# Batch norm with ReLU on one core: storing the second half of x by one DMA of 8 MB instead of two of 4 MB

## Chip, cores and metric

One core of a Trainium2 chip. The metric is device time in microseconds (us), median of several executions.

## The reference

```python
def reference(x, gamma, beta, running_mean, running_var, eps):
    normalized = (x - running_mean[None, :, None, None]) / np.sqrt(running_var[None, :, None, None] + eps)
    scaled = normalized * gamma[None, :, None, None] + beta[None, :, None, None]
    return np.maximum(scaled, 0).astype(np.float32)
```

x is 32 x 128 x 32 x 32 float32, 16.78 MB; the output is as large. Everything else is tiny.

## The kernel before

The 4096 rows (batch times channel) of 1024 numbers are cut into two halves `t`; in a half each of 128 partitions holds 16 consecutive rows `j`, 64 KB, contiguous in HBM. The sync queue loads pieces of a half; ScalarE applies scale, bias and ReLU in place, one row `j` (128 x 1024) an instruction; the scalar queue stores a piece when its rows are done. The scales and biases come from a short chain at the start, cut here.

```python
J = 16
PIECES = (((0, 2), (2, 4), (4, 8), (8, 16)), ((0, 8), (8, 16)))
STORE_CUTS = {(0, 1)}
# ...
    tiles = []
    for t in range(T):
        for a, b in PIECES[t]:
            xt = data.tile([P, b - a, HW], F32, name=f"x{t}_{a}")
            nc.sync.dma_start(out=xt, in_=xr[t, :, a:b, :])
            tiles.append((t, a, b, xt))
# ... scales and biases ...
    with tc.manual_schedule(engines={mybir.EngineType.Activation}):
        for t, a, b, xt in tiles:
            first = a
            for j in range(a, b):
                nc.scalar.activation(out=xt[:, j - a, :], in_=xt[:, j - a, :], func=ACTF.Relu,
                                     bias=bias_t[:, j : j + 1], scale=scale_t[:, j : j + 1])
                if j + 1 == b or (t, j + 1) in STORE_CUTS:
                    nc.scalar.dma_start(
                        out=outr[t, :, first : j + 1, :], in_=xt[:, first - a : j + 1 - a, :])
                    first = j + 1
```

A piece is called by its tile: x0_8 is rows 8 to 15 of the first half, x1_0 and x1_8 are the two pieces of the second. A DMA of n rows moves, on each partition, one run of n x 4 KB.

## Time and profile before

| | before |
|---|---|
| time, median of 3 | 83.86 us (83.7 to 83.93) |
| span of the profiled execution | 81.9 us |
| busy: ScalarE; every other engine | 47%; 1% or less |
| loads, stores | 16.78 MB each |
| share of 16 DMA engines: loads, stores | 48.4%, 47.8% |

The profile's lines are in the prediction, where they are read. Besides its views I use the records of single DMA packets: start, length, size and queue. In this kernel one packet of data is one run on one partition. A record does not name its engine: "on one engine" means packets that follow one another without a pause.

### The profile page before, as it was taken

The numbers are of one execution on the slowest core, as the hardware profiler recorded it, in microseconds if no ns is written. First come the engines' busy times: TensorE is split into PE (matmuls) and PEld (weight loads), VectorE is DVE, ScalarE is ACT, GpSimd is POOL, SyncE is SP. The second block draws the span as 40 slices with busy tenths as digits, with TensorE's granted clock in tenths as the row PEclk, the third lists the DMA queues.
The fourth block names the chain that finished last, engine by engine and source line by source line (L and its number), as shares of the span: only waits on it lengthen the run. The fifth ranks groups of instructions, "written<-read, shape, count | busy, mean of one in ns | idle before, by whom it ended". The sixth has DMA issues, their size and how long they took to land.

```text
span 81.9 us, 119 instructions
## 1 busy us (share of the span) xinstructions
PE 0.7 (1%) x2; PEld 0.5 (1%) x2; DVE 0.8 (1%) x5; ACT 38.5 (47%) x34; POOL 0.8 (1%) x6
## 2 busy tenths in 40 slices
PE   0002000000000000000000000000000000000000
PEld 0002000000000000000000000000000000000000
DVE  0000300000000000000000000000000000000000
ACT  0600377799039999199994199993000000000000
POOL 3000000000000000000000000000000000000000
DMA  2899999989899999979789798996999899799690
GB/s 32 328 425 472 408 448 448 512 352 494 370 448 416 446 418 396 500 296 600 320 380 580 304 464 384 512 512 288 480 512 400 368 512 448 320 512 496 272 512 0
DMA packets 1936, 33.56 MB, mean 410 GB/s; under 512 B 272, under 2 KB 272, under 8 KB 528
## 3 DMA queue, kind: packets, MB, share of 16 engines
q1 hardware_dynamic: 864, 16.78, 48.4%
q10 hardware_dynamic: 1072, 16.78, 47.8%
HBM read 16.78 MB, written 16.78 MB: 410 GB/s over the span
## 4 chain that ended last, share of the span: by engine, by line
DMA 56%; ACT 11%; SPq 0%; issue 0%
DMA x<-in_x_dram 56%; ACT x L96 11%; SPq L52 0%
## 5 line engine op out<-in xcount | busy, mean ns | idle before, releaser
L96 ACT ACTIVATE x<-x,bias_t,scale_t 128x1024 f32<-128x1024 f32 x32 | 37.0, 1228 | 10.3 <-DMA x<-in_x_dram 7.9
L82 ACT ACT_TABLE_LOAD x1 | 1.3, 1283 | 2.6 <-issue 2.6
L82 ACT ACTIVATE std_t<-cols,eps_t 128x16 f32<-128x16 f32 x1 | 0.3, 273 | 4.5 <-PE cols L74 4.5
L74 PE MATMUL cols<-raw,rep 8*128 8x64 f32 x2 | 0.7, 428 | 7.7 <-DMA raw<-in_beta_dram 7.7
L74 PEld LDWEIGHTS cols<-raw,rep 8*128 8x128 f32 x2 | 0.5, 304 | 7.7 <-issue 7.7
L64 POOL TENSOR_SCALAR_AFFINE_SELECT rep<-rep 8x128 f32<-8x128 f32 x1 | 0.4, 392 | 0.1
L84 DVE RECIPROCAL rstd_t<-std_t 128x16 f32<-128x16 f32 x1 | 0.3, 254 | 7.8 <-ACT std_t L82 7.8
L63 POOL MEMSET rep<- 8x128 f32 x1 | 0.2, 195 | 0.3 <-POOLq L124 0.3
L86 DVE TENSOR_TENSOR scale_t<-cols,rstd_t 128x16 f32<-128x16 f32 x1 | 0.2, 175 | 0.1
L90 DVE TENSOR_TENSOR bias_t<-cols,ms_t 128x16 f32<-128x16 f32 x1 | 0.2, 175 | 0.0
L88 DVE TENSOR_TENSOR ms_t<-cols,scale_t 128x16 f32<-128x16 f32 x1 | 0.2, 175 | 0.0
L124 POOL MEMSET const-bfloat16-1.0<- 128x1 bf16 x1 | 0.1, 106 | 0.0
L124 POOL MEMSET const-uint8-127<- 128x1 uint8 x1 | 0.1, 106 | 0.0
L124 POOL MEMSET const-float32-0.0<- 128x1 f32 x1 | 0.1, 103 | 0.3 <-issue 0.3
L124 POOL MEMSET const-float32-1.0<- 128x1 f32 x1 | 0.1, 103 | 0.0
L61 DVE MEMSET eps_t<- 128x1 f32 x1 | 0.1, 59 | 0.9 <-PEq L124 0.9
## 6 DMA issues: line engine op xcount, KB each, us to landing
x<-in_x_dram SPq DMA_DIRECT2D x3, 4096.0 KB, 38.8
out_dram<-x ACTq DMA_DIRECT2D x3, 4096.0 KB, 27.9
x<-in_x_dram SPq DMA_DIRECT2D x2, 1024.0 KB, 5.7
x<-in_x_dram SPq DMA_DIRECT2D x1, 2048.0 KB, 11.2
out_dram<-x ACTq DMA_DIRECT2D x1, 2048.0 KB
out_dram<-x ACTq DMA_DIRECT2D x2, 512.0 KB, 18.8
out_dram<-x ACTq DMA_DIRECT2D x1, 1024.0 KB
raw<-in_running_var_dram ACTq DMA_DIRECT2D x1, 0.5 KB
```

The lines of the kernel that those rows point to most:

```text
L61: nc.vector.memset(eps_t, float(eps))
L63: nc.gpsimd.memset(rep, 1.0)
L64: nc.gpsimd.affine_select(out=rep, in_=rep, compare_op=mybir.AluOpType.is_equal, fill=0.0, base=0, pattern=[[0, P // Q], [-1, Q]], channel ...
L74: nc.tensor.matmul(cols.rearrange("p k j -> p (k j)"), rep.rearrange("q r s -> q (r s)"), raw.rearrange("q k j -> q (k j)"), start=True, s ...
L82: nc.scalar.activation(out=std_t, in_=cols[:, 0, :], func=ACTF.Sqrt, bias=eps_t[:, 0:1], scale=1.0)
L84: nc.vector.reciprocal(out=rstd_t, in_=std_t)
L86: nc.vector.tensor_mul(out=scale_t, in0=cols[:, 1, :], in1=rstd_t)
L88: nc.vector.tensor_mul(out=ms_t, in0=cols[:, 2, :], in1=scale_t)
L90: nc.vector.tensor_sub(out=bias_t, in0=cols[:, 3, :], in1=ms_t)
L96: nc.scalar.activation(out=xt[:, j - a, :], in_=xt[:, j - a, :], func=ACTF.Relu, bias=bias_t[:, j : j + 1], scale=scale_t[:, j : j + 1],)
L124: nc = _bacc.Bacc("TRN2", target_bir_lowering=False, num_devices=1)
```

## The change

Its intent: store the second half with one DMA and longer runs (64 KB in place of 32), so fewer packets and one DMA fewer. The half becomes one tile; its two loads stay, each into a part of it. The store must now wait for all sixteen rows.

```diff
-PIECES = (((0, 2), (2, 4), (4, 8), (8, 16)), ((0, 8), (8, 16)))
+TILES = ((0, 0, 2), (0, 2, 4), (0, 4, 8), (0, 8, 16), (1, 0, 16))
 
+LOAD_CUTS = {(1, 8)}
 STORE_CUTS = {(0, 1)}
@@
-    for t in range(T):
-        for a, b in PIECES[t]:
-            xt = data.tile([P, b - a, HW], F32, name=f"x{t}_{a}")
-            nc.sync.dma_start(out=xt, in_=xr[t, :, a:b, :])
-            tiles.append((t, a, b, xt))
+    for t, a, b in TILES:
+        xt = data.tile([P, b - a, HW], F32, name=f"x{t}_{a}")
+        cuts = [a] + [j for j in range(a + 1, b) if (t, j) in LOAD_CUTS] + [b]
+        for c, d in zip(cuts, cuts[1:]):
+            nc.sync.dma_start(out=xt[:, c - a : d - a, :], in_=xr[t, :, c:d, :])
+        tiles.append((t, a, b, xt))
```

## The prediction

> **What bounds the kernel now.** I began with the page's busy shares, which rule the compute engines out: ScalarE (ACT) is busy 47% of an 81.9 us span, nothing else over 1%. The row of DMA slices and the two queue lines say what is full.
>
> ```profile
> DMA  2899999989899999979789798996999899799690
> DMA packets 1936, 33.56 MB, mean 410 GB/s; under 512 B 272, under 2 KB 272, under 8 KB 528
> q1 hardware_dynamic: 864, 16.78, 48.4%
> q10 hardware_dynamic: 1072, 16.78, 47.8%
> L96 ACT ACTIVATE x<-x,bias_t,scale_t 128x1024 f32<-128x1024 f32 x32 | 37.0, 1228 | 10.3 <-DMA x<-in_x_dram 7.9
> ```
>
> The two queues (q1 loads, q10 stores) fill 48.4 + 47.8 = 96.2% of 16 engines' time; only the first slice and the last one or two are empty. So bytes over rate set the time: 33.56 MB, which the change leaves alone. The question left is whether the changed stores let the engines run dry, make packets slower, or add a tail. The chain of waits names only the loads and the last eight activations, and shows when the second half is ready:
>
> ```profile
> 7.99 38.77 DMA x<-in_x_dram
> 46.76 0.03 issue
> 46.79 9.16 ACT x L96 x8
> ```
>
> Read it with care: it stops at 55.95 us although the span ends at 81.9, since nothing follows the last activation but transfer. The last 26 us are stores. For those I read the timeline (start, length, what) and the time to landing of single stores, asked for in windows around their issues at 33.05 and at 44.00 us:
>
> ```profile
> 33.05 0.34 ACTq L104 DMA_DIRECT2D out_dram<-x  x1
> 34.81 9.16 ACT L96 ACTIVATE x<-x,bias_t,scale_t 128x1024 f32<-128x1024 f32 x8 [1.79 <-DMA x<-in_x_dram]
> 44.00 0.34 ACTq L104 DMA_DIRECT2D out_dram<-x  x1
> 46.79 9.16 ACT L96 ACTIVATE x<-x,bias_t,scale_t 128x1024 f32<-128x1024 f32 x8 [2.82 <-DMA x<-in_x_dram]
> 55.97 0.34 ACTq L104 DMA_DIRECT2D out_dram<-x  x1
> ```
> ```profile
> out_dram<-x ACTq DMA_DIRECT2D x1, 4096.0 KB, 28.6
> ```
> ```profile
> out_dram<-x ACTq DMA_DIRECT2D x1, 4096.0 KB, 27.3
> ```
>
> The store of x0_8 (issued 33.05) lands at 33.05 + 28.6 = 61.65 us; that of x1_0 (issued 44.00) at 44.00 + 27.3 = 71.3. The first of x's second half thus sits in the queue for 61.65 - 44.34 = 17 us before its turn. The 4 MB between the landings took 9.65 us, 435 GB/s. The table by stretch (width, busy, clock, DMA share, GB/s) has the same rate for both stores:
>
> ```profile
> 51.60:61.30 9.70, 0.00 (x0) 0.00 (x0) 0.00 (x0) 4.34 (x4) 0.00 (x0) 1.00 1.00 432
> 61.30:71.00 9.70, 0.00 (x0) 0.00 (x0) 0.00 (x0) 0.00 (x0) 0.00 (x0) 1.00 1.00 432
> ```
>
> **What the Trainium skill says.** All of it is in "DMA: Bandwidth & Descriptors". (1) "Rules for kernel authors" asks for at least 1 MiB a DMA for bandwidth; the stores are 4 MiB already and run at 432, so size has no more to give. (2) "Why small descriptors are slow" puts a fixed cost of about 3 cycles on each packet. The packet records agree in kind: on one engine eight 16 KB packets took 4.857 us (607.1 ns each) and eight of 32 KB 9.676 us (1209.5 ns each), so a packet costs 2 x 607.1 - 1209.5 = 4.7 ns and the rest is bytes. (3) "Queues, rings and completion order" says that an engine goes round-robin between queues packet by packet; in the records 32 KB loads do alternate with single 4 KB or 8 KB store packets until the last load packet ends at 46.4 us. Larger store packets would take more of the engines from the loads, but only if they met. (4) "Latency and other measured facts" has copies slow down at row pitches of 512 KiB and more. Here the pitch in HBM is 16 x 4 KB = 64 KB before and after, and 432 GB/s shows no harm from it.
>
> **The change part by part.**
> The loads: the same six DMAs in the same order, the last two into halves of one tile. No term, provided that the activations of j = 0..7 wait for the first half alone. Whether dependencies follow regions or whole tiles can be read from the kernel before, where x0_0 has two stores: its first row is stored by the DMA issued at 10.99 us, which lands 14.2 us later, and the activation that writes its second row starts at 11.42. It didn't wait for a reader of another part. Likewise the four small loads write parts of one tile and are issued at 0.81, 1.43, 1.75 and 2.08 us without waiting for one another. I take regions.
>
> The activations: 16 as before, eight from 34.81 and eight from 46.79 us, the second eight gated by the load as now. Their end stays 55.95. Without the issue at 44.00 (0.34 us) ACT only waits longer for the load.
>
> The stores: the 4 MB at 44.00 goes; one of 8 MB comes at 55.97. The delay of the first half by 12 us costs nothing if the queue still has x0_8's packets: those last until about 61.3 us in the packet records (landing 61.65), 5.4 us after the issue. How long may an issue take to its first packet? The first load: 0.81 to 2.1 us, 1.3 us. The longest that I find: the first store, issued 10.99, first packet 14.93 us, 3.9 us, behind queued loads. Even that leaves 5.4 - 3.9 = 1.5 us. So no gap, and the new packets follow at 61.3.
>
> The bytes from there: 128 partitions over 16 engines is 8 rows an engine, now 8 packets of 64 KB in place of 16 of 32 KB. A 64 KB packet should take 2 x 1209.5 - 4.7 = 2414 ns; saved 8 x 4.7 = 38 ns, plus one completion record an engine at 6 ns: 44 ns in parallel on all engines, 0.04 us of time. If the run is cut back into 32 KB packets when lowered, about 0.01. The 64 KB packets start 15 us after the loads end, so point (3) has nothing to act on.
>
> The tail: the last packets end between 80.6 and 80.9 us now, then about 1 us to the end of the span. One final landing before, one after. No term; the spread may move by 0.1 or 0.2 us either way.
>
> Sum: 83.86 - 0.04 = 83.82 us.
>
> **The rivals.**
> (a) Dependencies go by whole tile after all: the first activation of the second half waits for the last load, 46.79 us; sixteen end at 46.79 + 9.16 x 2 = 65.1; store issued there, first packet 1.3 us later at the earliest, 66.4, against 61.3: a gap of 5.1 us, so about 89 us, +6%. Against it: the two observations above. I give it 4%.
> (b) The queue runs dry although regions hold, because of a long way from issue to first packet: it would have to exceed 5.4 us; 3.9 was the longest under load. Something between 84 and 85 us; 2%, mostly still within 2%.
> (c) Long packets pay or lose: if 64 KB packets were treated unlike 32 KB ones by 2% (an engine that reads a whole run before it writes, uneven finish of 16 engines), 19.4 us of stores change by 0.4 us: 83.4 or 84.2. The straight line from 4 KB (155.5 ns measured, 155.3 from the fit) to 32 KB speaks against it.
> (d) Fewer DMAs save fixed cost each: 1 to 2 us if DMAs of one queue ran one after another. Against: at the change from x0_8 to x1_0 the engine passes in 6 ns from one's last packet to the other's first; the cost is hidden already.
>
> **Range and chances.** Three runs of before spread 83.7 to 83.93; the effect is smaller than that. 83.6 to 84.1 covers the noise, (c) in part, and the small side of (b). Faster by 2% would mean 82.2, below what 33.56 MB at 432 GB/s (77.7 us) plus the start of 2.1, the end of 1.0 and 1.9 outside the span (83.77 - 81.9) allow: 82.7. So 1%. Slower by 2% is (a) and the rest of (b): 5%.
>
> **What would show it.** Right: activations of the second half from 34.8 and 46.8 us; one 8 MB store at about 56.0; the DMA row full through 56 to 63; 1936 - 128 - 16 = 1792 packets (1920 if the runs are cut in two); the last packets end at 80.6 to 80.9; span 81.8 to 81.9. Wrong: sixteen activations in a row from 46.8 (a), an empty slice near 61 us with a full row after it (b), a lower GB/s after 61 or engines ending far apart (c).

## The result

The changed kernel takes 83.89 us (83.76 to 84.03, 6 runs), the kernel before 83.88 in the same rounds. The ratio is 1.0002, 95% interval 0.9988 to 1.0016: the same. Ratios here are the mean time of one kernel's runs over that of the other's of the same rounds, so not quite the ratio of the quoted medians.

The page of the changed kernel, the lines that answer to those shown of before:

```profile
DMA  3799998989999997969889699997992899998290
DMA packets 1792, 33.56 MB, mean 410 GB/s; under 512 B 256, under 2 KB 256, under 8 KB 512
q1 hardware_dynamic: 864, 16.78, 48.7%
q10 hardware_dynamic: 928, 16.78, 47.7%
```

Same bytes, same rate, 96.4% of the engines' time in place of 96.2; 144 packets fewer, just the 128 of data and 16 completion records forecast. Short runs of low digits in the DMA row are no holes here: a packet is counted in the slice where it starts, and a 64 KB packet outlasts a slice of 2 us. The timeline of its second half (start, length, what):

```profile
33.13 0.34 ACTq L106 DMA_DIRECT2D out_dram<-x  x1
35.01 9.16 ACT L98 ACTIVATE x<-x,bias_t,scale_t 128x1024 f32<-128x1024 f32 x8 [1.91 <-DMA x<-in_x_dram]
46.89 9.16 ACT L98 ACTIVATE x<-x,bias_t,scale_t 128x1024 f32<-128x1024 f32 x8 [2.73 <-DMA x<-in_x_dram]
56.08 0.34 ACTq L106 DMA_DIRECT2D out_dram<-x  x1
```

The first eight activations still start when their own load lands, 12 us before the other's; the store at 44.0 is gone. The DMA issues with their time to landing (the 8 MB store's size is missing in the view):

```profile
out_dram<-x ACTq DMA_DIRECT2D x1, 4096.0 KB, 28.6
...
out_dram<-x ACTq DMA_DIRECT2D x1, 24.9
```

x0_8 lands at 33.13 + 28.6 = 61.73 us, the big store at 56.08 + 24.9 = 80.98. That is 19.25 us for 8.39 MB, 436 GB/s, where x1_0's store of before went at 435. In the packet records each engine passes from x0_8's last packet to its first 64 KB packet without a pause, the first engine at 61.0 us and the last at 61.4.

So the data of the first part waited: before, in the store queue behind x0_8; after, in SBUF, until the issue. What has to be tested is that this is the whole reason: that delay is free up to a limit, where the limit lies, and that the long run isn't quietly paying for a cost of the delay.

### The profile page after: what moved, and what is told of

Same layout as the page of the kernel before. It is cut to its first block, busy times and chain, and to the rows that moved or that the text cites. A ratio compares the mean times of both kernels' runs of the same rounds, so it can differ in the third digit from the quotient of the medians.

```text
span 81.9 us, 118 instructions
## 1 busy us (share of the span) xinstructions
PE 0.7 (1%) x2; PEld 0.5 (1%) x2; DVE 0.8 (1%) x5; ACT 38.5 (47%) x34; POOL 0.8 (1%) x6
## 2 busy tenths in 40 slices
DMA packets 1792, 33.56 MB, mean 410 GB/s; under 512 B 256, under 2 KB 256, under 8 KB 512
## 4 chain that ended last, share of the span: by engine, by line
DMA 56%; ACT 10%; issue 2%; SPq 0%
DMA x<-in_x_dram 56%; ACT x L98 10%; SPq L54 0%
## 6 DMA issues: line engine op xcount, KB each, us to landing
out_dram<-x ACTq DMA_DIRECT2D x1, 4096.0 KB, 28.6
```

## The experiments

My theory: the engines are bound by bytes, and an issue of the store costs nothing while the queue holds older stores, which it does until 61.0 us on the first engine and 61.4 on the last. Rivals: delay and long run each have an effect and cancel; or the time of issue does not matter at all.

**e1: compute the two halves in the other order.** Every activation of the half now waits for the last load.

```diff
-            for j in range(a, b):
+            order = list(range(8, 16)) + list(range(0, 8)) if t == 1 else list(range(a, b))
+            for j in order:
```

(The store follows the last of `order` and covers the whole tile as before.)

> The two halves of x1 are computed in the other order, so that all sixteen activations wait for the last load (46.9 us) and the one 8 MB store is issued at about 46.9 + 18.3 = 65.2 us, 3.9 us after the queue's last packet of x0_8 (61.3). Same bytes, same packets as the changed kernel; only the issue is later. Theory (the delay is free only as long as the store queue holds older bytes): a gap from 61.3 to 65.2 plus the way from issue to first packet; with 1.3 us for that (read at the first load) 5.2 us, so 89.1 us; with 3.9 us (the longest read) 91.7. Rival (the time of issue hardly matters, because the sixteen engines catch up or the end is set elsewhere): under 85.5 us.

Measured: 88.67 us, ratio 1.0568. The timeline of e1:

```profile
46.78 18.21 ACT L99 ACTIVATE x<-x,bias_t,scale_t 128x1024 f32<-128x1024 f32 x16 [13.76 <-DMA x<-in_x_dram]
65.02 0.34 ACTq L108 DMA_DIRECT2D out_dram<-x  x1
```

and its table by stretch (start and end, width, busy time of PE, PEld, DVE, ACT, POOL, clock, DMA share, GB/s), followed by that of the changed kernel:

```profile
60.00:62.00 2.00, 0.00 (x0) 0.00 (x0) 0.00 (x0) 2.00 (x3) 0.00 (x0) 1.00 0.04 16
62.00:64.00 2.00, 0.00 (x0) 0.00 (x0) 0.00 (x0) 2.00 (x3) 0.00 (x0) 1.00 0.00 0
```
```profile
60.00:62.00 2.00, 0.00 (x0) 0.00 (x0) 0.00 (x0) 0.00 (x0) 0.00 (x0) 1.00 1.37 590
62.00:64.00 2.00, 0.00 (x0) 0.00 (x0) 0.00 (x0) 0.00 (x0) 0.00 (x0) 1.00 1.21 524
```

The hole is there in e1 and not in the changed kernel (whose shares over 1 come from counting a packet where it starts). When the store's packets come, the DMA view of e1 from 61 to 67 us shows, in 40 slices of 0.15 us:

```profile
GB/s 0 0 0 0 0 0 0 0 0 0 0 0 0 0 0 0 0 0 0 0 0 0 0 0 0 0 0 0 0 0 0 0 5680 1311 0 0 0 0 0 0
```

They start from 65.80 us on; by the packet records the first starts at 65.86, 0.84 us after the start of the issue (the expectation of e5 has 66.20 and 1.18). The engines stand idle 4.82 us on average; the time rose by 4.8. The issue does matter, once it is late enough. This is also what the prediction's rival (a), dependencies by whole tile, would have looked like; the estimate there was 89.

**e2 and e5: find the limit.** Extra activations on a scratch tile stand ahead of the store, four in e2 and six in e5.

```diff
+    scratch = params.tile([P, HW], F32, name="scratch")
@@
+                if (t, j) == (1, 15):
+                    for _ in range(4):          # 6 in e5, 1 in e11
+                        nc.scalar.activation(out=scratch, in_=xt[:, 0, :], func=ACTF.Relu)
                 if j + 1 == b or (t, j + 1) in STORE_CUTS:
```

> Four extra activations of 1.15 us on a scratch tile delay the 8 MB store from 56.1 to about 60.7 us, still 0.6 us before the queue runs out at 61.3. Theory: the gap is 60.7 + L - 61.3, where L is the way from issue to first packet. L = 1.3 us gives a gap of 0.7 and 84.6 us; L = 2 gives 1.4 and 85.3; L = 3.9 gives 3.3 and 87.2. Rival (an issue ahead of the queue's end is always in time): 83.9 us, no gap.

Measured: 83.63 us and no gap. The expectation of a gap failed: the store went out at 59.17, not 60.7, as its timeline shows.

```profile
55.91 4.30 ACT L108 ACTIVATE scratch<-x 128x1024 f32<-128x1024 f32 x4
59.17 0.34 ACTq L110 DMA_DIRECT2D out_dram<-x  x1
```

The issue came as the last extra activation began, not as it ended; I had put it too late, mostly by one activation. So 3.1 us of delay beyond the changed kernel's cost nothing. That the time is a little *under* before's was unexpected; e9 to e11 return to it.

> As e2, with six extra activations. In e2 each held the store back by about 1.08 us except that the store went out as the last one began (issued 59.17 us, not 60.7, and there was no gap). Six should put the issue at 59.17 + 2 x 1.08 = 61.3 us, just when the queue runs out. e1 measured 1.18 us from issue to first packet (65.02 to 66.20). Theory: first 64 KB packet at 62.5, a gap of 1.1 to 1.2 us, 85.0 us. Rival (there is no threshold, e2 was free for another reason): 83.7 us.

Measured: 84.89 us, ratio 1.0119. Its timeline and one stretch:

```profile
55.87 6.48 ACT L108 ACTIVATE scratch<-x 128x1024 f32<-128x1024 f32 x6
61.30 0.34 ACTq L110 DMA_DIRECT2D out_dram<-x  x1
```
```profile
60.00:62.00 2.00, 0.00 (x0) 0.00 (x0) 0.00 (x0) 1.94 (x3) 0.00 (x0) 1.00 0.08 33
```

First packet at 62.14 us, 0.84 after the issue began; engines idle 1.12 us, as forecast. From e5 to e1 the issue moves by 3.72 us and the time by 3.78: past the limit, between these two points, every us of delay is a us of time. Together:

| kernel | store issued | first 64 KB packet | idle before it | time |
|---|---|---|---|---|
| changed | 56.08 | 60.98 | none | 83.89 |
| e2 | 59.17 | 60.94 | none | 83.63 |
| e5 | 61.30 | 62.14 | 1.12 | 84.89 |
| e1 | 65.02 | 65.86 | 4.82 | 88.67 |

The limit is the queue's end on the first engine less the way from issue to packet: 61.0 - 0.84 = about 60.1 us (the shift of 0.3 us in the recorded texts drops out of it), an inference between the two measured points 59.17 and 61.30. The change had 4.0 us to spare.

**e3 and e6: the delay without the long run.** The tile stays one, but two stores of 4 MB are issued after the last activation.

```diff
-                    nc.scalar.dma_start(
-                        out=outr[t, :, first : j + 1, :], in_=xt[:, first - a : j + 1 - a, :]
-                    )
+                    step = 8 if t == 1 else j + 1 - first
+                    for f in range(first, j + 1, step):        # e6: reversed(range(...))
+                        nc.scalar.dma_start(
+                            out=outr[t, :, f : f + step, :], in_=xt[:, f - a : f - a + step, :]
+                        )
```

> Tile, loads and time of issue as in the changed kernel, but two stores of 4 MB with 32 KB runs, both issued after the last activation: the delay without the long run. Theory: 0.04 us over the changed kernel, not resolved by timing, 83.9 us, with 16 more data packets an... in all 128 more packets of data and 16 more completion records (1792 + 144 = 1936). Rival (the delay costs and the long runs give it back, or the other way round): a difference from before of 0.5 us or more either way.

Measured: 84.03 us, ratio 1.0007 (0.999 to 1.0024). But the run doesn't test what it was made for. Its timeline:

```profile
47.05 1.24 ACT L98 ACTIVATE x<-x,bias_t,scale_t 128x1024 f32<-128x1024 f32 x1 [3.06 <-DMA x<-in_x_dram]
47.13 0.34 ACTq L108 DMA_DIRECT2D out_dram<-x  x1
48.20 8.01 ACT L98 ACTIVATE x<-x,bias_t,scale_t 128x1024 f32<-128x1024 f32 x7
56.24 0.34 ACTq L108 DMA_DIRECT2D out_dram<-x  x1
```

The store of the first eight rows stands after sixteen activations in the program, yet went out when the second eight had just begun. The Trainium skill's page "Advanced Engine Details and Errata", section "Sequencer Loop", describes a sequencer that pushes engine instructions into a queue and reads on; this trace agrees, with seven activations overtaken. That store was delayed by 3 us, not 12. In e2 and e5, by contrast, a store whose data were ready stayed behind the extra activations. There each extra starts 0.03 us after the one before has ended, while the activations of e3 overlap a little; whether that makes the difference was not tested. e6 mends it: the store that must wait stands first.

> e3 mended: there the store of the first half, whose data were ready, went out at 47.13 us and was not delayed to 56. Here the store of the second half, which must wait for the last activation, stands first in the program, so both 4 MB stores are issued from 56.1 us. The delay without the long run. Theory: no gap at 61.3, 1936 packets, 83.9 us, the ratio to before within 0.3% of 1. Rival (the delay alone costs and the 64 KB run gives it back): 84.3 us or more.

Measured: 83.90 us, ratio 1.0011 (0.9994 to 1.0027), both stores late:

```profile
56.08 1.57 ACTq L108 DMA_DIRECT2D out_dram<-x  x2
```

With the delay and without the long run the time is the same as with both (1.0002) and as with neither. A cost of the delay paid back by the long run would have to be under 0.3%, the top of the interval.

**e4: much shorter runs.** As e3, with `step = 1`: sixteen stores of 512 KB in runs of 4 KB.

> As e3, but sixteen stores of 512 KB with 4 KB runs, issued one after the other from 56.1 us (0.34 us each, so always ahead of the engines, which need 1.2 us for one). Theory (4.7 ns a packet and 6 ns a completion record): an engine moves 128 packets at 155.5 ns and 16 records = 20.0 us in place of 8 x 2414 ns = 19.3 us; + 0.7 us, 84.6 us. Rival one (run length means nothing): 83.9. Rival two (each DMA pays a fixed 1 to 2 us in turn): 100 us or more.

Measured: 84.44 us, ratio 1.0068 (1.0051 to 1.0086), +0.57 us against the 0.7 expected. The stores weren't issued as planned: seven went out between 46.99 and 54.83 us, as in e3; the other nine from 62.12, about 1.2 us apart. By the semaphores in the trace each of the nine waited for the landing of the store eight before it (62.05 us for the first, x0_8), as eight DMA semaphores are used in turn. The queue stayed ahead of the engines all the same: the records show no hole over 0.03 us in any microsecond from there to the end, and 420 GB/s between 62.2 and 80 where long runs had 432. At that rate 8.39 MB take 20.0 us in place of 19.4, the 0.6 measured. So the packet cost of some 5 ns is real, 16 times more packets for this half than after the change are needed to see 0.7%, and one DMA more or less does not add a microsecond when DMAs queue.

**e7 and e8: the same merge where loads are under way.** In e7 the first half is stored by one DMA of 8 MB and the second by two; in e8 both halves by one.

```diff
-TILES = ((0, 0, 2), (0, 2, 4), (0, 4, 8), (0, 8, 16), (1, 0, 16))
-LOAD_CUTS = {(1, 8)}
-STORE_CUTS = {(0, 1)}
+TILES = ((0, 0, 16), (1, 0, 8), (1, 8, 16))      # e8: ((0, 0, 16), (1, 0, 16))
+LOAD_CUTS = {(0, 2), (0, 4), (0, 8)}             # e8: and (1, 8)
+STORE_CUTS = set()
```

> The same merge made on the first half of x instead, where loads are still under way: one store of 8 MB with 64 KB runs issued at about 33 us, the second half stored in two as in the kernel before. Loads keep their sizes and order. Theory (queues alternate packet by packet): each 32 KB load packet of 1.21 us now waits for a 64 KB store packet of 2.41, so the loads end not at 46.7 but between 51 (3.9 us from issue to first packet) and 59 us (1.2 us). Yet the queue of stores then holds enough to cover it: no gap, same bytes, 83.8 us. Rival (an end of loads later by 5 to 12 us moves the end of the kernel by as much): 89 to 95.

Measured: 84.78 us, ratio 1.0102. Its timeline:

```profile
32.19 9.16 ACT L98 ACTIVATE x<-x,bias_t,scale_t 128x1024 f32<-128x1024 f32 x8 [0.55 <-DMA x<-in_x_dram]
...
57.70 9.16 ACT L98 ACTIVATE x<-x,bias_t,scale_t 128x1024 f32<-128x1024 f32 x8 [16.35 <-DMA x<-in_x_dram]
```

The last load landed at 57.7 us instead of 46.9: loads do give way when a 64 KB store packet stands between two of theirs (on one engine in the records: 1213 ns load, 2418 ns store, in turn, once the first stretched load packets are through). And an end of loads later by 11 us didn't move the end by 11 us, as the store queue had enough to cover it; the rival is refuted. But 0.9 us were lost that my theory did not foresee. In the packet records some load packets took longer than 1213 ns, up to 2741. Those over by more than 50 ns start between 31.6 and 36.8 us, that is from the first store's issue at 31.67 to just after its first packet at 36.16. Summed over all 32 KB load packets the excess is 1.47 us an engine, against 0.36 in the changed kernel: 1.1 us more. That this is the lost time is argued from its size alone; why they stretch is open.

> e7 and the change together: one 8 MB store for each half. Theory: the late loads of e7 and the late issue of the change meet: the first store's packets end at about 61, the second store is issued 9.9 us after the loads' end at 51 to 59, so at 61 to 69, and its first packet comes at 62.5 to 70. A gap of 1.2 (loads end at 51) to 9 us (at 59): 85 to 92 us. Rival (merging either half is free, so both together are): 83.9.

Measured: 90.34 us, ratio 1.0767. The DMA row of its page and its timeline:

```profile
DMA  2999998999969996959959939990009999909990
```
```profile
57.79 9.16 ACT L98 ACTIVATE x<-x,bias_t,scale_t 128x1024 f32<-128x1024 f32 x8 [16.26 <-DMA x<-in_x_dram]
66.98 0.37 ACTq L106 DMA_DIRECT2D out_dram<-x  x1
```

The three zeros are the hole, 5.9 us of idle engines ahead of a first packet at 67.8. Late loads alone cost 1%, a late store alone nothing, both together 7.7%: the merge of the second half is free only because the first half's stores are cut small while loads run.

**e12: take the two loads away too.** `LOAD_CUTS = set()`: the second half loaded by one DMA.

> What the change kept is taken away: the second half is loaded by one DMA of 8 MB, 64 KB runs, too. Theory: the load's 64 KB packets alternate with 8 KB store packets, so the loads end earlier, about 44.2 us (46.7 before), but all sixteen activations wait for that: the store is issued at 44.4 + 18.2 = 62.6 us, its first packet comes 1.2 us later, 63.8, against an empty queue from 61.3: a gap of 2.5 us (up to 3.1), 86.4 to 87.0 us. Rival (a load that ends earlier helps the end): 83.9 or less.

Measured: 87.01 us, ratio 1.0372, at the top of what was expected. Its timeline:

```profile
45.19 18.20 ACT L98 ACTIVATE x<-x,bias_t,scale_t 128x1024 f32<-128x1024 f32 x16 [12.12 <-DMA x<-in_x_dram]
63.43 0.34 ACTq L106 DMA_DIRECT2D out_dram<-x  x1
```

The load landed 1.7 us earlier than in the changed kernel (I had put it at 2.5), but sixteen activations followed it where eight did, and the engines stood idle for 2.6 us. "Its loads stay two" is what keeps the change free.

**e9, e10, e11: the odd 0.3%.** Five rounds each of the changed kernel, of e2, and of e2 with one extra activation.

> The changed kernel unaltered, five rounds, beside e10 and e11. In e2 four extra activations came out at 83.63 us, 0.3% under the kernel before (interval 0.9953 to 0.9985), which no theory had foreseen. Theory: the changed kernel and the kernel before are equal, 83.9 us, ratio within 0.2% of 1.

> e2 again, five rounds. If its 0.3% was chance of the few executions: 83.9 us here, ratio 0.998 to 1.001. If it is real: 83.6 and 0.997 again, with the changed kernel of e9 at 1.000.

> One extra activation in place of four: the scratch tile is allocated as in e2, so that every tile lies where it does there, but the store goes out at its old time, about 56 us. If e2's gain is real and comes from where the tiles lie, 83.6 us here too; if it came from the later store, 83.9; if chance, 83.9 here and in e10.

Measured: e9 83.92 us, ratio 1.0008 (0.9992 to 1.0023); e10 83.66, 0.9969 (0.9956 to 0.9982); e11 83.69, 0.9977 (0.9963 to 0.999). So it is no chance, and it isn't the later store: e11 issued at 56.03 us. What e10 and e11 share is the scratch tile and at least one more activation.

The record says more, as every execution has its span (from first to last instruction) beside its time. Means over all executions:

| kernel (executions) | span | time less span |
|---|---|---|
| before (33) | 82.02 | 1.89 |
| delay, two stores: e3, e6 (12) | 82.10 | 1.88 |
| changed: the result and e9 (12) | 81.88 | 2.05 |
| e2, e10 (10) | 81.85 | 1.81 |
| e11 (6) | 81.83 | 1.90 |

So the odd 0.3% is not a faster run inside the span: the kernels that store the second half by one DMA without a gap all have about the same span, under that of those with two. The changed kernel differs by the time that it takes outside the span, 0.16 us more than before. The spread of that time, from 1.69 us (e8) to 2.07 (e9) by kernel, stays open, and with it what the scratch tile or the activation has to do with it. At 0.3%, e2 is the fastest version seen, but that is below 2%, and not a gain of the change.

## Why the prediction was right

- **Dependencies by region**: right. The first eight activations start at 35.01, the second at 46.89. That x0_0's second row was written while its first was being stored had told it.
- **Time of issue** 55.97: measured 56.08, with the loads 0.1 us later in that execution (46.9).
- **Room before the queue runs dry**: right in size; x0_8's packets end from 60.9 us before and from 61.0 after. (61.3 - 55.97 is 5.3, not the 5.4 written.) The way from issue to first packet was left between 1.3 and 3.9 us, on the profile's clock 1.0 and 3.65; behind an empty queue it is 0.84 to 0.87 (e1, e5, e8, e12). The long figure came from a packet that had loads ahead of it. With the short one the room was 4.0 us, not 1.5. Rival (b) was further off than stated.
- **Packets**: 1792, as said; a 64 KB packet every 2414 ns on an engine in the records, as worked out from the 16 and 32 KB ones.
- **The saving of 0.04 us**: not resolved. The two measurements of the changed kernel, 1.0002 and 1.0008, have intervals of 0.14 to 0.16% either side, three times the effect. Only e4 shows the packet cost in time, multiplied. The sum also took the time outside the span as fixed at 1.9 us; it rose by 0.16 (1.89 to 2.05) while the span fell by 0.14 (82.02 to 81.88). That the time is the same to 0.01 us is thus in part luck: two effects, each larger than the one forecast, that cancel.
- **Point (3), no meeting with the loads**: right, and e7 shows what it is worth when they meet.
- **The tail**: the last data packets end at 80.3 to 80.7 us, before at 80.3 to 80.6 (the 80.6 to 80.9 of the prediction has the shift of 0.3). But "no term" was wrong by more than the saving forecast: from the last landing to the end of the span the profiled executions take 0.93 us in before, e3 and e6, and 0.83 in the changed kernel, e1, e2, e5, e9, e10 and e11. At the end SyncE waits for the stores in a fixed order. With two stores for the second half, the one that lands last is not the last in that order, and two more waits follow it, 0.06 us apart; with one store none does. That is 0.10 of the 0.14 us by which the span fell; the rest is within its noise.
- **Rival (c)**: refuted for finish and rate, 436 GB/s. **Rival (d)**: refuted at its 1 to 2 us by e6, one DMA more at the same time.

The median, 83.89, is 0.07 over the 83.82 forecast and within the range. The mechanism, transfer time unchanged and the delay hidden behind older stores, is what the runs show; the hundredths are not.

## What to carry to other kernels

In a kernel bound by transfer, ask of a late store not when its data are ready but when the queue would have reached it: delay is free up to the queue's end less the way from issue to first packet (0.84 us here), and costs a us for each us beyond. Merging transfers from runs of 32 KB to 64 KB paid next to nothing here: about 5 ns a packet and 0.1 us of waits at the end. It is safe at the end of a stream, if the queue holds enough before it, not where another queue waits its turn behind the long runs. To delay a DMA in an experiment, give it data that are late: its place in the program alone held it back in e2 and e5, but not in e3. And look at the span beside the time: effects of 0.1 us inside and outside it can cancel.

## What the Trainium skill lacked or had wrong

- "DMA: Bandwidth & Descriptors", "Latency and other measured facts", gives about 600 ns to the first byte for DMAs issued from sync or scalar, but not from when it counts. Here 0.84 to 0.87 us passed from the start of the issue to the first packet at an idle queue (e1, e5, e8, e12), about 0.5 us from the end of the issue instruction of 0.34 to 0.37; the figure lies between.
- The same page, "Queues, rings and completion order", measures an engine's turn in packets of several descriptors. Here a turn was one run, whatever its length, up to 64 KB and 2418 ns, and the other queue paid for it: loads done at 57.7 us instead of 46.9 (e7). "Rules for kernel authors" recommends large DMAs without this warning.
- No page that I read has it: load packets stretch, from 1213 to as much as 2741 ns, between a store's issue and its first packets, 1.1 us an engine in all (e7 against the changed kernel).
- No page that I read has it: the time less the span differs between kernels of one task, from 1.69 us (e8) to 2.07 (e9); cause open. At the end each wait for a landed store takes about 0.06 us (before, e6).
